# The gated half of the mixed rows: turned by VectorE inside the attention, stored and reloaded turned, with the sums of W_out's blocks moved into the projections

## The chip, the cores and the metric

The kernel runs on one core of one Trainium2 chip. The metric is the device time of one execution in microseconds (us), the median over several. Engines are named as in the profile: PE (TensorE, with PEld for its weight loads), DVE (VectorE), ACT (ScalarE), POOL (GpSimd) and SP (SyncE, which issues most of the DMAs).

## The reference, cut to what matters

One decoder layer over S = 2048 tokens of width D = 1024, all in float32:

```
n = rmsnorm(x);  proj = n @ W_in      # gated q, k, v, gate, low-rank; dilated q, k, v
o_a = gated linear attention, 4 heads of 128, normalised per head, * g * silu(gate)    # S x 512
o_b = dilated attention, 8 heads of 64, three (window, dilation) branches              # S x 512
h = x + [o_a ; o_b] @ W_out
h = h + relu(rmsnorm(h) @ W_ff1)**2 @ W_ff2
y = rmsnorm(h)
```

The change touches how `o_a` travels from the attention to the product with W_out, and where sums of W_out's rows are made for that product.

## The kernel before, in words

**Arithmetic.** Every large product splits both float32 operands into a high part (fp32r) and the rest, and takes three matmuls (`mm3`, L139 to L142). Most products are Strassen-like: seven block products `j` in place of eight, on sums of blocks made by DVE (and by POOL for some weights).

**Stages.** (1) Projections: column groups of W_in, first for tokens 0 to 1023 and then for 1024 to 2047. The loop at L849 runs 126 jobs (group, block product); a group takes seven. A group of 128 columns is "chained" (block products share a PSUM bank) and takes 12 matmuls of 512 columns per job. `prep` (L291) makes a job's weight parts two jobs ahead: ACT writes the high part (L304), DVE the low part (L306, L308), and DVE also makes the sums of blocks (L310 to L316). `load_w` (L284) fetches the next group's weights, through SP for chained groups. `second_half` normalises the second 1024 tokens beside it and turns them with DVE's 32 x 32 block transpose (`squares`, L605); a DMA then puts the blocks in place when they are reloaded (`load_turned`).

(2) Attention: a loop over 160 units of the dilated branches (scores, softmax, transposes, values), PE issuing three units ahead. `gla_steps` (L1161), the gated linear attention, is a generator that is advanced about every second unit; it takes tokens in tiles of 128. In the kernel before, the tokens inside a tile lie in the order 0, 16, 32, ... 1, 17, ... (8 by 16, the function `_order`), and `token_rows` (L144) puts the result rows back in natural order when they are stored in `mixD`. Also in this stage `sum_wo` (L1251, four generators of six steps) loads two row blocks of W_out, has ACT scale the first by the norm's gain (L1257), has POOL make four differences of 128 x 512 (L1261) and stores them in `wtD`.

(3) Product with W_out: `load_mix` (L1467) reads pairs of row tiles from `mixD`; `mix_block` (L1485) turns a row tile by four PE transposes per 512 columns (L1491), so eight for a tile of 1024. The first four row tiles go through `plain_rows` (L1668, ACT and DVE split the turned tile straight from PSUM); for the other twelve, `raw_block` (L1618) has ACT copy the turned tile to SBUF (L1623), `prep0` (L1625) makes the operand parts three jobs ahead, and `product0` (L1654) runs the seven block products of a pair, 12 matmuls each, and has DVE add the result to the residual row (L1664). `row_done` (L1642) stores the row in `hD` and queues `norm_row` (L1410): square and sum on ACT, a scale on DVE that overwrites the row in place (L1415), eight PE transposes (L1420), two ACT copies (L1421), a store in `hTD`.

(4) The MLP's two products, about 1160 us, which the change touches only by calls of `turn_rows`.

**What sets the order.** Each engine runs its instructions in a fixed order, written at compile time by a scheduler that simulates the program: an instruction is placed when, in the simulation, its operands are ready, earlier program lines first. `keep_in_program_order` pins an instruction behind the one traced before it on its engine. SBUF is one pool of 25 slots (`slot`, L127) which tiles take and give back.

## Time and profile before

| | us |
|---|---|
| runs: median of 3 | 2221.89 |
| lowest, highest | 2221.43, 2228.46 |
| the profiled execution | 2219.28 |
| its span, first to last instruction | 2217.1 |

The profiled execution is 2.2 us longer than its span, and 2.6 us under the median. In the profile "busy" counts the time in which an engine has an instruction running; PE's matmuls overlap one another, so what a matmul costs PE is the distance between its start and the next one's, not its duration. A group's row has count, busy time, mean ns of one, and the idle time of the engine just before those instructions with what ended it.

### The profile page before, as it was taken

To read this page: it belongs to the slowest core of one execution; us is meant where nothing else is said; L and a number is where in the kernel's file an instruction comes from. 1 tells how busy PE (TensorE), PEld (TensorE's weight loads), DVE (VectorE), ACT (ScalarE), POOL (GpSimd) and SP (SyncE) were. 2 spreads that over 40 slices of the span, in tenths; PEclk is the share of its full clock that TensorE was granted. 3 is DMA by queue.
4 is the path that set the end of the run, shared out by engine and by line. 5 is a ranking of instruction groups with operands and counts; after the bars stand their busy time and mean duration, and the time that the engine had idled before them with its cause. 6 is when DMAs were issued, how large, how long until landed. Compare 5 with 4: busy or idle time off the path is not lost.

```text
span 2217.1 us, 34928 instructions
## 1 busy us (share of the span) xinstructions
PE 2198.8 (99%) x12356; PEld 1910.1 (86%) x12356; DVE 1662.0 (75%) x3100; ACT 1231.3 (56%) x2406; POOL 604.8 (27%) x653
## 2 busy tenths in 40 slices
PE   9999999999999999999999999999999999999998
PEld 8988998899999998888888888888888888888886
DVE  8677766757777887769776778767786697576788
ACT  7364424537888884547555566555555433333446
POOL 1000300135577672000000000000008443042672
PEclk9999999999999999999999999999999999999999
DMA  6576965777967976868654456555499998677875
GB/s 208 174 218 209 253 204 187 241 243 266 313 231 229 293 262 232 264 212 273 187 167 133 150 180 182 156 177 155 133 299 279 305 297 273 213 258 244 270 263 183
DMA packets 325074, 499.88 MB, mean 225 GB/s; under 512 B 21479, under 2 KB 226938, under 8 KB 313636
## 3 DMA queue, kind: packets, MB, share of 16 engines
q1 hardware_dynamic: 285426, 336.35, 46.8%
q0 software_dynamic: 32128, 108.61, 17.2%
q10 hardware_dynamic: 7346, 52.70, 6.4%
q8 instruction: 97, 1.59, 0.3%
q14 instruction: 77, 0.63, 0.1%
HBM read 339.45 MB, written 162.85 MB: 227 GB/s over the span
## 4 chain that ended last, share of the span: by engine, by line
PE 76%; issue 12%; DMA 4%; DVE 4%; ACT 2%; POOL 1%; SPq 1%; DVEq 0%; POOLq 0%; ACTq 0%
PE ps_a L141 7%; PE ps_a L140 7%; PE ps_a L142 7%; PE ps_c L141 7%; PE ps_c L140 7%; PE ps_c L142 7%; PE ps_a L1021 4%; PE ps_d L141 4%; PE ps_d L142 4%; PE ps_d L140 4%; PE ps_o L140 3%; PE ps_o L141 3%; PE ps_o L142 3%; PE ps_d L1002 3%; PE ps_c L984 2%
## 5 line engine op out<-in xcount | busy, mean ns | idle before, releaser
L543 ACT ACTIVATE cb<-bs 128x1024 fp32r<-128x1024 f32 x104 | 110.2, 1060 | 284.4 <-PE ps_o L141 99.9
L544 DVE TENSOR_TENSOR cb<-bs,cb 128x1024 fp32r<-128x1024 f32 x104 | 150.6, 1449 | 129.0 <-ACT cb L543 128.6
L1508 POOL DMA_DIRECT2D w1raw<-w_ff x64 | 48.0, 750 | 700.3 <-DVE mcomb L544 522.7
L544 DVE TENSOR_TENSOR mcomb<-w1raw,mcomb 128x512 fp32r<-128x512 f32 x224 | 153.4, 685 | 91.4 <-ACT mcomb L543 91.4
L1798 POOL TENSOR_TENSOR bs<-bs,rb 128x1024 f32<-128x1024 f32 x60 | 167.3, 2789 | 199.9 <-DMA bs<-w_ff 196.3
L543 ACT ACTIVATE mcomb<-w1raw 128x512 fp32r<-128x512 f32 x224 | 140.5, 627 | 80.0 <-PE ps_c L142 27.3
L1021 PE MATMUL ps_a<-v,pt 128*128 128x65 f32 x1200 | 177.4, 253 | 2.5 <-ACT pt L1009 1.5
L1021 PEld LDWEIGHTS ps_a<-v,pt 128*128 128x128 f32 x1200 | 172.7, 194 | 4.3 <-ACT pt L1009 1.9
L993 ACT ACTIVATE pe<-pe,O 128x256 f32<-128x256 f32 (+1 forms) x384 | 156.2, 453 | 14.0 <-DVE O L992 11.6
L1002 PE MATMUL ps_d<-ident,pe 128*128 128x128 f32 x600 | 158.4, 279 | 0.2 <-ACT pe L993 0.2
L304 ACT ACTIVATE wcomb<-wraw 128x512 fp32r<-128x512 f32 (+2 forms) x119 | 90.3, 759 | 117.4 <-PE ps_a L141 45.5
L992 DVE CUSTOM_DVE_ANT_0 pe<-ps_c,nb 128x256 f32<-128x256 f32 (+1 forms) x384 | 126.5, 360 | 37.6 <-PE ps_d L1002 18.4
L544 DVE TENSOR_TENSOR ca<-ra,ca 128x1024 fp32r<-128x1024 f32 x84 | 133.6, 1592 | 0.2 <-ACT ca L543 0.2
L140 PE MATMUL ps_c<-hb,mcomb 128*128 128x512 f32 x320 | 124.8, 390 | 0.3 <-ACT xs L1588 0.3
L141 PE MATMUL ps_c<-hb,mcomb 128*128 128x512 f32 x320 | 124.5, 389 | 0.0
L142 PE MATMUL ps_c<-hb,mcomb 128*128 128x512 f32 x320 | 124.2, 389 | 0.0
L140 PE MATMUL ps_c<-cb,ca 128*128 128x512 f32 x312 | 121.4, 389 | 0.0
L141 PE MATMUL ps_c<-cb,ca 128*128 128x512 f32 x312 | 121.4, 389 | 0.0
L142 PE MATMUL ps_c<-cb,ca 128*128 128x512 f32 x312 | 121.4, 389 | 0.0
L1002 PEld LDWEIGHTS ps_d<-ident,pe 128*128 128x128 f32 x600 | 108.3, 185 | 0.6 <-ACT pe L993 0.3
L306 DVE TENSOR_TENSOR wcomb<-wraw,wcomb 128x512 fp32r<-128x512 f32 (+2 forms) x77 | 72.8, 945 | 48.0 <-ACT wcomb L304 47.9
L1579 ACT ACTIVATE acc<-acc 128x512 f32<-128x512 f32 x96 | 60.7, 632 | 79.5 <-DVE acc L1598 37.1
(497 smaller groups left out, 7241.5 us busy)
## 6 DMA issues: line engine op xcount, KB each, us to landing
ra<-actD ACTq DMA_DIRECT2D x50, 1024.0 KB, 7.7
actD<-ring SPq DMA_DIRECT2D x176, 256.0 KB, 3.1
rb<-w_ff POOLq DMA_DIRECT2D x84, 512.0 KB, 6.4
bs<-w_ff SPq DMA_DIRECT2D x72, 512.0 KB, 5.8
w1raw<-w_ff POOLq DMA_DIRECT2D x64, 512.0 KB, 5.2
k<-kD SPq DMA_DIRECT2D x16, 1024.0 KB, 8.0
rb<-hTD SPq DMA_DIRECT2D x28, 512.0 KB, 5.5
wraw<-w_in SPq DMA_DIRECT2D x48, 256.0 KB, 4.0
```

The costliest lines, as they stand in the source:

```text
L140: T.matmul(out, sh, mh, start=first, stop=False, **kw)
L141: T.matmul(out, sl, mh, start=False, stop=False, **kw)
L142: T.matmul(out, sh, ml, start=False, stop=last, **kw)
L304: A.activation(hi, src, AF.Copy, scale=sc)
L306: V.tensor_tensor(lo, src, hi.bitcast(F32), op=OP.subtract)
L543: A.activation(hi, src, AF.Copy)
L544: V.tensor_tensor(lo, src, hi.bitcast(F32), op=OP.subtract)
L992: V.tensor_tensor_reduce(p, s, bias, scale=1.0, scalar=BIG, op0=OP.add, op1=OP.min, accum_out=nm)
L993: A.activation(p, p, AF.Exp, bias=nm, scale=-1.0)
L1002: T.transpose(pb[:, i * 128:i * 128 + 128], src, ident)
L1021: T.matmul(self.b.opsum[:, n % 4], self.pt[:, i * 128:i * 128 + 128], self.b.v[:, blk, cols], start=first, stop=last)
L1798: (engines or ((G,), (V, V))[len(sums) - 1])[e].tensor_tensor(v, v, r, op=OP.add if op == "+" else OP.subtract)
```

## The change

1. The gated attention now works in natural token order inside a tile: `gla_load` and `gla_load_v` read the rows of the gate, v and output gate through `natural_rows`, the constants lose `_order`, and the projected gated q and k (`gq`, `gk`) are put in natural order when they leave PSUM, with the strided form that `dq` had already.
2. At the end of a tile DVE turns the 128 x 512 result in 32 x 32 blocks (`squares`); it is stored in 512-byte runs in the new `mixD`, two tensors of 128 x 16 x 256. The dilated half keeps its natural rows in a tensor of its own, `mixN`.
3. `load_mix` reads the gated half with four DMAs per pair, one for each 32 partitions, in 1 KB runs, which finishes the transposition, and the dilated half with two. The gated half is used from SBUF as it lies (`gated_of`, a strided view); `mix_block` and `raw_block` turn only the dilated half.
4. `sum_wo` moves to the second half of the projections, one generator of four steps per row block on one slot, advanced at the jobs in `SUMS_WO`: 85, 88, 89, 90, then 91, 94, 95, 96, and so on to 108. Its loads are pinned on SP, POOL does the scaling, and POOL issues the store.
5. `norm_row` writes its result in `scr`, not over the row; its transposes are queued and issued by `turn_rows`, called after a block product.

The diff, changed lines with little context:

```diff
@@ -29,6 +29,7 @@
+SUMS_WO = [a + k for a in (85, 91, 97, 103) for k in (0, 3, 4, 5)]
@@ -218,7 +219,8 @@
-    mixD = dram.tile([S, D], F32, name="mixD")
+    mixD = [dram.tile([128, 16, 256], F32, name=f"mixD{h}") for h in range(2)]
+    mixN = dram.tile([S, 512], F32, name="mixN")
@@ -466,7 +468,7 @@
             q = p[:, :m]
-            if kind == "dq":
+            if kind in ("dq", "gq", "gk"):
@@ -844,7 +846,27 @@
+    wtD = dram.tile([4, 128, 2 * D], F32, name="wtD")
+    def sum_wo():
+        raw = slot("wtsum")
+        for c in range(4):
+            for k in range(2):
+                tc.keep_in_program_order(SP.dma_start(raw[:, D * k:D * k + D], wo[:, c + 4 * k]))
+            yield
+            G.tensor_tensor(raw[:, :D], raw[:, :D], gn[:, c:c + 1].to_broadcast([128, D]), op=OP.mult)
+            yield
+            b11, b12, b21, b22 = [raw[:, 512 * k:512 * k + 512] for k in range(4)]
+            for n, (dst, x, y) in enumerate(((b12, b12, b11), (b22, b22, b12), (b21, b21, b22), (b11, b22, b11))):
+                G.tensor_tensor(dst, x, y, op=OP.subtract)
+                if n == 1:
+                    yield
+            G.dma_start(wtD[c], raw[:, :2 * D])
+            yield
+    of_sums = sum_wo()
@@ -863,6 +885,8 @@
             back.pop(0)()
+        if at in SUMS_WO:
+            next(of_sums)
@@ -1080,7 +1104,7 @@
-                        mixD[:, 512 + 128 * pr:640 + 128 * pr].rearrange("(t p) n -> p t n", p=128)[:, ts],
+                        mixN[:, 128 * pr:128 * pr + 128].rearrange("(t p) n -> p t n", p=128)[:, ts],
@@ -1124,18 +1148,21 @@
+    def natural_rows(ap, t, row):
+        return bass.AP(tensor=ap.tensor, offset=ap.offset + t * 128 * row, ap=[[row, 8], [8 * row, 16], [1, row]])
-            SP.dma_start(gst["g"][t % 2], glD[tk])
+            SP.dma_start(gst["g"][t % 2], natural_rows(glD, t, 256))
-            tk = slice(t * 128, t * 128 + 128)
-            SP.dma_start(gst["gv"][t % 2], gvD[tk])
-            SP.dma_start(gst["sr"][t % 2], srD[tk])
+            SP.dma_start(gst["gv"][t % 2], natural_rows(gvD, t, 512))
+            SP.dma_start(gst["sr"][t % 2], natural_rows(srD, t, 512))
@@ -1204,8 +1231,11 @@
             yield
-            V.tensor_tensor(o, o, view(sg, (4, 128)), op=OP.mult)
-            issue_later(4, token_rows(mixD, t, D, width=512), o.rearrange("p h e -> p (h e)"))
+            V.tensor_tensor(view(sg, (4, 128)), o, view(sg, (4, 128)), op=OP.mult)
+            flat = o.rearrange("p h e -> p (h e)")
+            squares(flat, sg)
+            issue_later(4, mixD[t // 8][:, t % 4 * 4:t % 4 * 4 + 4, t % 8 // 4 * 128:t % 8 // 4 * 128 + 128],
+                        view(flat, (4, 128)))
@@ -1246,23 +1276,6 @@
-    wtD = dram.tile([4, 128, 2 * D], F32, name="wtD")
-    def sum_wo(c):
-        raw = slot("wtsum")
-        for k in range(2):
-            SP.dma_start(raw[:, D * k:D * k + D], wo[:, c + 4 * k])
-        yield
-        A.activation(raw[:, :D], raw[:, :D], AF.Copy, scale=gn[:, c:c + 1])
-        yield
-        b11, b12, b21, b22 = [raw[:, 512 * k:512 * k + 512] for k in range(4)]
-        for n, (dst, x, y) in enumerate(((b12, b12, b11), (b22, b22, b12), (b21, b21, b22), (b11, b22, b11))):
-            G.tensor_tensor(dst, x, y, op=OP.subtract)
-            if n < 3:
-                yield
-        issue_later(4, wtD[c], raw[:, :2 * D])
-        yield
@@ -1354,9 +1367,6 @@
-    sums_wo = [x for c in range(4) for x in [sum_wo(c)] * 6]
-    for n, x in enumerate(sums_wo):
-        at_unit(8 + AHEAD + 2 * n, next, x)
@@ -1400,7 +1410,7 @@
-    norms = []
+    norms, turning = [], []
@@ -1412,14 +1422,20 @@
-        V.scalar_tensor_tensor(h, h, r, gM, op0=OP.mult, op1=OP.mult)
-        k = t % HT // 4
-        for q in range(2):
-            pv = view(ps("c"), (4, 128))
-            for c in range(4):
-                T.transpose(pv[:, c], h[:, (4 * q + c) * 128:(4 * q + c + 1) * 128], ident)
-            A.activation(hb4[2 * k + q], pv, AF.Copy)
-        store_T(t, *(((1, 0), (2, 1)) if k == 0 else ((3, 3),)))
+        V.scalar_tensor_tensor(scr, h, r, gM, op0=OP.mult, op1=OP.mult)
+        turning.append(t)
+    def turn_rows():
+        while turning:
+            t = turning.pop(0)
+            k = t % HT // 4
+            for q in range(2):
+                pv = view(ps("c"), (4, 128))
+                for c in range(4):
+                    T.transpose(pv[:, c], scr[:, (4 * q + c) * 128:(4 * q + c + 1) * 128], ident)
+                A.activation(hb4[2 * k + q], pv, AF.Copy)
+            store_T(t, *(((1, 0), (2, 1)) if k == 0 else ((3, 3),)))
@@ -1466,12 +1482,23 @@
-            u = mxs[p] = view(slot("mx"), (2, D))
+            u = slot("mx")
+            mxs[p] = view(u[:, :1024], (4, 256)), view(u[:, 1024:], (2, 512))
+            half, i = divmod(p, 4)
+            to = 384 if half == 0 else 512
+            for g in range(4):
+                m = mixD[half][:, 4 * i + g]
+                SP.dma_start(mxs[p][0][32 * g:32 * g + 32], bass.AP(
+                    tensor=m.tensor, offset=m.offset, ap=[[16 * 256, 32], [32 * 16 * 256, 4], [1, 256]]))
-                to = D - 128 if t < 8 else D
-                for cs in (slice(0, 512), slice(512, to)) if p == 0 else (slice(0, to),):
-                    SP.dma_start(u[:, e, cs], mixD[t * 128:t * 128 + 128, cs])
+                SP.dma_start(mxs[p][1][:, e, :to], mixN[t * 128:t * 128 + 128, :to])
+    def gated_of(p, e):
+        return mxs[p][0].rearrange("p g (e c t) -> p e c g t", e=2, t=32)[:, e]
+    def by_quarter(v):
+        return v.rearrange("p c (g t) -> p c g t", g=4)
@@ -1482,13 +1509,13 @@
-    def mix_block(p, e, q, tag):
+    def mix_block(p, e):
-        pv = view(ps(tag), (4, 128))
+        pv = view(ps("c"), (4, 128))
-            of = mxs[p][:, e, (4 * q + k) * 128:(4 * q + k + 1) * 128]
-            T.transpose(pv[:, k], outs[3, 0][:, t, 1:129] if t < 8 and 4 * q + k == 7 else of, ident)
+            T.transpose(pv[:, k], outs[3, 0][:, t, 1:129] if t < 8 and k == 3 else mxs[p][1][:, e, 128 * k:128 * k + 128],
+                        ident)
@@ -1615,12 +1642,12 @@
-    def raw_block(p, e, q):
+    def raw_block(p, e):
-                raw0.append(view(slot("ar"), (4, 4, 128)))
-            A.activation(raw0[0][:, 2 * e + q], mix_block(p, e, q, "c"), AF.Copy)
+                raw0.append(view(slot("ar", n=1024), (2, 4, 128)))
+            A.activation(raw0[0][:, e], mix_block(p, e), AF.Copy)
@@ -1629,9 +1656,10 @@
-        a11, a12, a21, a22 = [raw0[0][:, n] for n in range(4)]
+        a11, a21 = [gated_of(g // 7, e) for e in range(2)]
+        a12, a22 = [by_quarter(raw0[0][:, e]) for e in range(2)]
-        split(c[:, 0], c[:, 1], {1: a11, 2: a12, 6: a11, 5: a21, 7: a11, 3: a12, 4: a22}[j])
+        split(by_quarter(c[:, 0]), by_quarter(c[:, 1]), {1: a11, 2: a12, 6: a11, 5: a21, 7: a11, 3: a12, 4: a22}[j])
@@ -1647,6 +1675,7 @@
     def next_norm():
+        turn_rows()
@@ -1667,8 +1696,8 @@
-        for q in range(2):
-            split(*[m[:, i, 4 * q:4 * q + 4] for i in range(2)], mix_block(p, e, q, "c"))
+        split(*[by_quarter(m[:, i, :4]) for i in range(2)], gated_of(p, e))
+        split(*[m[:, i, 4:] for i in range(2)], mix_block(p, e))
@@ -1687,8 +1716,8 @@
         if at == 3:
-            for n in range(4):
-                raw_block(2, n % 2, n // 2)
+            for e in range(2):
+                raw_block(2, e)
@@ -1702,6 +1731,7 @@
         next_norm()
+        turn_rows()
@@ -1710,16 +1740,15 @@
         product0(g)
+        turn_rows()
             load_x(p + 1)
-            raw_block(p + 1, 0, 0)
-            raw_block(p + 1, 1, 0)
         if i == 3:
-            raw_block(p + 1, 0, 1)
+            raw_block(p + 1, 0)
         if i == 4:
-            raw_block(p + 1, 1, 1)
+            raw_block(p + 1, 1)
@@ -1888,6 +1917,7 @@
         product1(at)
+        turn_rows()
@@ -1938,11 +1968,6 @@
-def _order():
-    r, i = np.divmod(np.arange(128), 8)
-    return 16 * i + r
@@ -1955,7 +1980,7 @@
-    o = _order()
+    o = np.arange(128)
```

## The prediction

> **What bounds the kernel now.** I read the page first, then the busy time by stage, then PE's own rows where a transposition meets matmuls.

> ```profile
> PE 2198.8 (99%) x12356; PEld 1910.1 (86%) x12356; DVE 1662.0 (75%) x3100; ACT 1231.3 (56%) x2406; POOL 604.8 (27%) x653
> ...
> PE 76%; issue 12%; DMA 4%; DVE 4%; ACT 2%; POOL 1%; SPq 1%; DVEq 0%; POOLq 0%; ACTq 0%
> ```

> PE has work 99% of the time, and most of the chain that ended last is PE. The three stages that the change touches (late projections, attention, product with W_out) are alike in that; the columns are the stretch, its length, then busy time and count for PE, PEld, DVE, ACT, POOL:

> ```profile
> 304.00:505.00 201.00, 201.00 (x1220) 180.34 (x1218) 125.34 (x196) 82.21 (x145) 27.22 (x35) 1.00 0.70 220
> 505.00:842.00 337.00, 334.03 (x3049) 328.52 (x3049) 262.51 (x1050) 291.72 (x845) 239.70 (x321) 1.00 0.82 271
> 842.00:1050.00 208.00, 206.42 (x1029) 171.58 (x1029) 163.98 (x255) 109.19 (x213) 10.53 (x16) 1.00 0.74 239
> ```

> PE idles 0, 3.0 and 1.6 us in them; the granted clock is 1.00. So what leaves PE's queue shortens the kernel, and what is added on other engines costs only where it makes PE wait.

> **The transpositions that go.** A matmul's duration is no price, since matmuls overlap; the price is from start to start. This is one group of eight transposes inside the product with W_out:

> ```profile
> 961.56 1.03 PE L1420 MATMUL ps_c<-ident,xh 128*128 128x128 f32 x8
> ...
> 962.35 0.48 PE L140 MATMUL ps_o<-wo,mcomb 128*128 128x512 f32 x1
> ...
> 962.66 0.40 PE L140 MATMUL ps_a<-wb,mcomb 128*128 128x512 f32 x1
> ...
> 962.90 0.39 PE L141 MATMUL ps_a<-wb,mcomb 128*128 128x512 f32 x1
> 963.13 0.39 PE L142 MATMUL ps_a<-wb,mcomb 128*128 128x512 f32 x1
> ```

> Eight take 962.35 - 961.56 = 0.79 us, 0.099 each. The first matmul after them takes 0.31 to the next start against the usual 0.23, so a group costs 0.08 more however long it is. (Twelve of 0.23 make a product of 2.7 us.) The mixed rows' transposes are of the same form:

> ```profile
> L1491 PE MATMUL ps_c<-ident,mx x120: 270/273/273, 835.8 to 1005.4; 128*128 128x128 f32 x120
> ...
> L1491 PE MATMUL ps_c<-ident,O x8: 270/273/331, 839.6 to 909.9; 128*128 128x128 f32 x8
> ```

> 128 in all, eight for each of 16 row tiles. Half go: 64 x 0.099 = 6.3 us. In the loop over pairs they stand at three places per pair (i = 2, 3, 4) and after the change at two, so six pairs save six groups, 0.5 us. Nothing on PE takes their place. That is 6.8 us.

> [...]

> **What takes over the turning.** DVE's transposition stands in the trace, for 128 x 1024:

> ```profile
> L607 DVE STREAM_TRANSPOSE bp<-xp 128x1024 f32<-128x1024 f32 x8 | 9.9, 1235 | 0.0
> ```

> Half of it, 0.62 us, for 16 tiles is 9.9 us of DVE in the attention, where DVE idles 337 - 262.5 = 74 us and the gated part runs ahead of its use. I take nothing for it; if that cover failed it would cost up to those 9.9 us. The rest is hidden too: the store in 512-byte runs (pair 0 needs only tiles 0 and 4, finished long before), and the reload with six DMAs per pair:

> ```profile
> L1474 SPq DMA_DIRECT2D mx<-mixD x18: 319/423/642, 827.3 to 959.4; - x18
> ...
> DMA to landing us min/median/max: 4.6/5.0/5.3
> ```

> 48 issues in place of 18, 30 x 0.42 = 13 us of SP's queue spread over some 200; they land in 5 us and are issued a pair ahead (seven products). The stores and loads of x behind them on SP slip by about 1.7 us per pair; they too are used a pair later. The twelve ACT copies from PSUM that go (two per pair) are off the path: ACT is busy 109 of 208 us there.

> **Natural order of gq and gk.** Their 28 evictions become strided. The strided form of dq stands in the same rows as the longest value:

> ```profile
> L482 ACT ACTIVATE acc<-ps_a x24: 577/600/1095, 111.9 to 453.9; 128x512 f32<-128x512 f32 x24
> ...
> L492 DVE TENSOR_TENSOR acc<-ps_c,acc x18: 672/692/1067, 112.9 to 451.1; 128x512 f32<-128x512 f32 x18
> ```

> So 0.5 us more on ACT (16 times), 0.4 on DVE (12 times). The bank is written again a whole product later, so PE doesn't see it: 0, at the worst 13 us if all of it lay bare.

> **The norm of h.** The scale no longer overwrites the row, so it no longer waits for the row's store:

> ```profile
> L1415 DVE SCALAR_TENSOR_TENSOR xh<-xh,stats,gs 128x1024 f32<-128x1024 f32 x16 | 20.5, 1280 | 15.9 <-DMA hD<-xh 12.7 <-ACT bb L1421 2.8 <-ACT mcomb L543 0.3
> ...
> L1420 PE MATMUL ps_c<-ident,xh 128*128 128x128 f32 x128 | 16.9, 273 | 0.7 <-DVE xh L1415 0.7
> ```

> 12.7 us of DVE's waiting go; PE waited for it once, 0.7 us. With the transposes queued behind the next product, that goes: 0.7 us. The new wait is that the next row's square may not write `scr` before these transposes have read it; the squares of two rows are two products, 5.4 us, apart and the transposes one product behind the scale, so ACT, where the splits queue behind the square, is not held.

> **The sums leave the attention.** There they cost PE one visible stall:

> ```profile
> 601.19 1.15 ACT L1257 ACTIVATE wtsum<-wtsum,stats 128x1024 f32<-128x1024 f32 x1 [1.25 <-DMA wtsum<-w_out]
> ...
> 602.42 2.65 POOL L1261 TENSOR_TENSOR wtsum<-wtsum 128x512 f32<-128x512 f32 x2 [2.33 <-ACT wtsum L1257]
> ...
> 604.00 1.61 DVE L1207 TENSOR_TENSOR gla<-gla 128x512 f32<-128x512 f32 x1 [1.24 <-ACT gla L1205]
> ...
> 606.94 0.43 PE L1021 MATMUL ps_a<-v,pt 128*128 128x65 f32 x2 [0.76 <-DVE pt L1011]
> ```

> ACT waits for a W_out block, DVE's 128 x 512 operation takes 1.61 us beside POOL's subtraction, and the copy behind it reaches PE late. 0.8 us go.

> **The sums enter the projections.** Per row block POOL does one 128 x 1024 product and four 128 x 512 differences:

> ```profile
> L1798 POOL TENSOR_TENSOR bs<-bs,rb 128x1024 f32<-128x1024 f32 x60 | 167.3, 2789 | 199.9 <-DMA bs<-w_ff 196.3 <-DVE cb L544 3.1
> L1261 POOL TENSOR_TENSOR wtsum<-wtsum 128x512 f32<-128x512 f32 x16 | 20.8, 1315 | 10.2 <-ACT wtsum L1257 10.0
> ```

> 2.8 + 4 x 1.3 = 8 us, four times, 32 us. POOL itself is free there (27 of 201 us). The question is DVE, which makes weight parts beside it, and how early they are:

> ```profile
> L1207 DVE TENSOR_TENSOR gla<-gla x16: 674/718/1606, 546.1 to 840.1; 128x512 f32<-128x512 f32 x16
> ...
> 389.28 0.68 DVE L308 SCALAR_TENSOR_TENSOR wcomb<-wraw,wcomb 128x512 fp32r<-128x512 f32 x1
> ...
> 391.07 0.39 PE L140 MATMUL ps_c<-tb,wcomb 128*128 128x512 f32 x1
> 391.30 0.39 PE L141 MATMUL ps_c<-tb,wcomb 128*128 128x512 f32 x1
> ```

> A DVE operation with both inputs in SBUF that meets POOL takes up to 1.61 in place of 0.67 us. The low part above is done at 389.96 and used at 391.30, 1.3 us early; this is the second job of a group, the tightest. In 8 us DVE is busy 8 x 125/201 = 5.0 us; if two thirds of that are SBUF operations and each doubles, 3.3 us come on top of 3.0 us of slack: nearly level. Bounds: 0, and, if DVE gets none of its SBUF work done while POOL runs, 8 - 3.0 - 1.3 = 3.7 us per block, 15 in all. I take 1.0, near the lower end.

> **The sum.** -6.8 - 0.7 - 0.8 + 1.0 = -7.3 us. The profiled execution took 2219.3 us (span 2217.1 and 2.2 around it), so 2212.0; the median of the runs is 2.6 above that execution, which makes 2214.6.

> **The rivals.**

> *POOL and DVE collide in the projections.* For: the 1.61 us above, and leads of 1.3 us. Against: DVE idles 76 us of the stage and only two jobs of a group are so tight. Between the bounds, about 9 us of stalls: 2221.9 - 8.3 + 9 = 2222.6, no change. [...]

> *SP stands behind a pinned load (the slower case).* One slot serves all four blocks, so block c + 1's load on SP waits until block c's store has landed, and weights of the next group queue behind it on SP:

> ```profile
> 407.62 0.69 DVE L310 TENSOR_TENSOR wraw<-wraw 128x512 f32<-128x512 f32 x1 [1.44 <-DMA wraw<-w_in]
> ```

> ```profile
> wtD<-wtsum SPq DMA_DIRECT2D x4, 1024.0 KB, 8.0
> ...
> wsum<-w_out POOLq DMA_DIRECT2D x4, 512.0 KB, 5.6
> ```

> DVE waits for W_in's blocks already. Load, POOL and store take 5.6 + 8 + 8.0 = 21.6 us per block; the jobs give it six products, 16.3 us. SP would stand 5.3 us for each of three blocks, and if the delay adds up 5.3, 10.6 and 15.9; less 1.3 us of lead each, 12 to 28 us. I price it at the middle, 20: 2221.9 - 8.3 + 20 = 2233.6. It decides where SP waits over 1.3 us with W_in's loads behind, and makes the kernel slower by over 0.3% from 15 us of stalls on. Against: the scheduler places a load when its simulated store has landed, so only its error counts.

> *More than the sum.* The attention loses all its 3.0 us of idle PE and the W_out product its 1.6, with no collision: 2221.9 - 6.8 - 4.6 = 2210.5.

> **How the numbers follow.** A difference of 0.3% (6.7 us, about what a measurement of this kernel can tell from no change) lies just inside my forecast. Chances: the forecast (2211 to 2218) 0.54, collision 0.20, SP's queue 0.14, more than the sum 0.12. Faster by over 0.3% is below 2215.2: 0.12 and three quarters of 0.54, 0.52. Slower is above 2228.6: four fifths of SP's case and a tenth of the collision's, 0.13. The rest, 0.35, is no change. The range 2208 to 2228 leaves out most of SP's case (0.12) and some of the best (0.05).

> **What would show it.** In the changed profile: 64 transposes at the dilated half's line, in groups of four; 16 block transposes of 0.62 us in the attention; no wait for hD's store before the norm's scale; POOL some 32 us busier in the late projections. The product with W_out should be 7 to 8 us shorter, the late projections as long as now. It is wrong if PE shows idle time there that ended with DVE's low parts (collision) or with W_in's loads behind a held SP (queue), or if the attention is over 2 us longer.

## The result, and the profile after

The changed kernel takes 2246.45 us (median of 5 runs, 2243.05 to 2247.61), the kernel before 2222.73 beside it: a ratio of 1.0103, 95% interval 1.0089 to 1.0116. It is 1.0% slower; the forecast was 2214.6 us, 0.3% faster. The profiled execution took 2247.61 us with a span of 2245.8, 28.7 more than before.

The line of busy time and the one of shares by engine of the chain that ended last, of the kernel after:

```profile
PE 2203.6 (98%) x12292; PEld 1912.0 (85%) x12292; DVE 1682.0 (75%) x3116; ACT 1231.0 (55%) x2390; POOL 615.1 (27%) x661
...
PE 72%; issue 14%; DMA 5%; POOL 3%; DVE 3%; ACT 2%; SPq 0%; POOLq 0%; DVEq 0%; ACTq 0%
```

PE has 64 instructions fewer and yet 4.8 us more busy time, and it idles 2245.8 - 2203.6 = 42.2 us instead of 18.3. So there are two questions: who leaves PE 23.9 us more idle, and what makes fewer instructions take longer. The three stages in the same columns as before, now ending at 511, 869 and 1077:

```profile
304.00:511.00 207.00, 202.96 (x1219) 179.99 (x1219) 137.13 (x196) 84.34 (x145) 62.22 (x59) 1.00 0.77 250
511.00:869.00 358.00, 341.11 (x3037) 336.16 (x3037) 268.27 (x1064) 288.98 (x836) 214.09 (x302) 0.96 0.75 231
869.00:1077.00 208.00, 203.87 (x985) 168.36 (x985) 166.46 (x259) 109.49 (x212) 12.75 (x20) 1.00 0.78 246
```

The projections are 6 us longer, the attention 21 us, and its granted clock, 1.00 before, is 0.96. In the third stage PE has 44 instructions fewer for the same 208 us. Around one wait in the attention the clock is seen at work (same columns, a stretch up to the wait's middle and the one behind it), with the matmul that waited:

```profile
785.00:788.20 3.20, 1.11 (x11) 0.92 (x10) 0.62 (x1) 0.00 (x0) 3.20 (x5) 1.00 1.13 277
788.20:798.50 10.30, 8.77 (x45) 8.77 (x46) 5.97 (x27) 7.24 (x20) 7.31 (x15) 0.50 0.38 120
```

```profile
785.21 0.33 PE L1045 MATMUL ps_a<-v,pt 128*128 128x65 f32 x2
785.38 0.28 PE L1026 MATMUL ps_d<-ident,pe 128*128 128x128 f32 x1
785.50 0.61 PE L1172 MATMUL ps_o<-gla 128*128 128x130 f32 x4
789.73 0.69 PE L1045 MATMUL ps_a<-v,pt 128*128 128x65 f32 x2 [3.62 <-DVE pt L1035]
790.21 0.42 PE L1026 MATMUL ps_d<-ident,pe 128*128 128x128 f32 x1
790.43 0.53 PE L1045 MATMUL ps_a<-v,pt 128*128 128x65 f32 x2
790.75 0.42 PE L1026 MATMUL ps_d<-ident,pe 128*128 128x128 f32 x1
```

PE waits 3.62 us, and from then on two values matmuls take 0.32 us to the next start (790.43 to 790.75) where they took 0.17 (785.21 to 785.38). The granted clock is 0.50 for 10.2 us. There are five such stretches in the changed kernel (behind waits at 516, 786, 815, 854 and 1113 us) and none in the kernel before, apart from the very end of both. PE is busy 23.5 us in them, of which half, 11.8 us, is put down to the clock (an estimate from its 0.50). That closes the account: PE's busy time is -6.8 + 11.8 = +5.0 (measured +4.8), its idle time +23.9, together 28.7.

The stages by their own landmarks (start of the matmul named, from the traces; times from the span's start):

| kernel | projections' last | W_out's first | W_out's last | FF1's last | span |
|---|---|---|---|---|---|
| before | 504.7 | 842.0 | 1032.5 | 1647.8 | 2217.1 |
| after | 510.6 | 869.3 | 1053.0 | 1677.0 | 2245.8 |
| norm alone | 504.0 | 841.1 | 1030.5 | 1644.7 | 2215.3 |
| turning alone | 503.6 | 846.3 | 1036.1 | 1654.9 | 2226.8 |
| sums' move alone | 506.7 | 851.5 | 1044.3 | 1660.7 | 2231.5 |
| all but the sums' move | 505.0 | 846.2 | 1031.5 | 1656.9 | 2227.3 |

W_out, first to last, is 190.5 us before and 183.7 after: the 6.8 us of the prediction are there. They are lost ahead of it and behind it: the projections are 5.9 us longer, the attention (from the projections' last to W_out's first) 21.4 us, and FF1, the MLP's first product (from W_out's last to its own last), 8.7 us.

The projections first. Beside POOL's sums (first fence) DVE's 128 x 512 operations (second) take 1.7 us in place of 0.69, and the low part of L308 reaches PE late (third):

```profile
408.19 2.07 POOL L858 TENSOR_TENSOR wtsum<-wtsum,stats 128x1024 f32<-128x1024 f32 x1 [5.37 <-DMA wtsum<-w_out]
410.35 6.72 POOL L862 TENSOR_TENSOR wtsum<-wtsum 128x512 f32<-128x512 f32 x4
```

```profile
412.56 1.67 DVE L318 TENSOR_TENSOR wraw<-wraw 128x512 f32<-128x512 f32 x1
414.15 1.78 DVE L312 TENSOR_TENSOR wraw<-wraw 128x512 f32<-128x512 f32 x1
415.86 1.76 DVE L308 TENSOR_TENSOR wcomb<-wraw,wcomb 128x512 fp32r<-128x512 f32 x1
```

```profile
417.67 0.50 PE L142 MATMUL ps_o<-tb,wcomb 128*128 128x512 f32 x1 [1.22 <-DVE wcomb L308]
```

This is the collision that the prediction priced; the six waits of the stage, five of them ended by DVE, are PE's 4.0 us of idle time in its row above. What it had not seen comes 50 us later, in POOL's queue (first fence), ACT's (second) and PE's (third):

```profile
456.53 2.28 POOL L858 TENSOR_TENSOR wtsum<-wtsum,stats 128x1024 f32<-128x1024 f32 x1 [2.90 <-DMA wtsum<-w_out]
458.88 5.60 POOL L862 TENSOR_TENSOR wtsum<-wtsum 128x512 f32<-128x512 f32 x4
464.78 0.57 POOL L865 DMA_DIRECT2D wtD<-wtsum  x1 [0.30 <-POOL wtsum L862]
465.35 1.55 POOL L286 DMA_DIRECT2D wraw<-w_in  x2
```

```profile
473.12 1.06 ACT L306 ACTIVATE wcomb<-wraw 128x1024 fp32r<-128x1024 f32 x1 [8.14 <-DMA wraw<-w_in]
```

```profile
515.47 0.40 PE L1026 MATMUL ps_d<-ident,pe 128*128 128x128 f32 x2
521.25 0.48 PE L1006 MATMUL ps_c<-k,qp 128*128 128x128 f32 x1 [5.38 <-POOL qp L959]
```

POOL issues the W_in blocks of the last group (256 columns wide). Two of the four stand behind the last block of sums and go out at 465 us; before, the last went out at 458.7. ACT, in order, stands 8.1 us for them; its later evictions, their stores and SP's loads of the bias tables come late, POOL packs q late, and PE waits 5.4 us at the attention's start and then runs 6.8 us at half clock. How much of that wait is due to POOL's queue, e6 and e8 below test.

### The profile page after: what moved, and what is told of

It reads as the page before. It is cut to its first block, busy times and chain, and to the rows that moved or that the text cites. A ratio compares the mean times of both kernels' runs of the same rounds, so it can differ in the third digit from the quotient of the medians.

```text
span 2245.8 us, 34844 instructions
## 1 busy us (share of the span) xinstructions
PE 2203.6 (98%) x12292; PEld 1912.0 (85%) x12292; DVE 1682.0 (75%) x3116; ACT 1231.0 (55%) x2390; POOL 615.1 (27%) x661
## 4 chain that ended last, share of the span: by engine, by line
PE 72%; issue 14%; DMA 5%; POOL 3%; DVE 3%; ACT 2%; SPq 0%; POOLq 0%; DVEq 0%; ACTq 0%
PE ps_a L143 7%; PE ps_a L142 7%; PE ps_a L141 7%; PE ps_c L143 6%; PE ps_c L142 6%; PE ps_c L141 6%; PE ps_a L1045 4%; PE ps_d L142 4%; PE ps_d L141 4%; PE ps_d L143 4%; PE ps_o L141 3%; PE ps_o L143 3%; PE ps_o L142 3%; PE ps_d L1026 3%; PE ps_c L1008 2%
## 5 line engine op out<-in xcount | busy, mean ns | idle before, releaser
L546 DVE TENSOR_TENSOR cb<-bs,cb 128x1024 fp32r<-128x1024 f32 x104 | 157.4, 1515 | 133.5 <-ACT cb L545 133.0
L1045 PE MATMUL ps_a<-v,pt 128*128 128x65 f32 x1200 | 182.1, 255 | 10.7 <-ACT pt L1033 5.2
L1045 PEld LDWEIGHTS ps_a<-v,pt 128*128 128x128 f32 x1200 | 177.6, 197 | 12.7 <-ACT pt L1033 5.4
L306 ACT ACTIVATE wcomb<-wraw 128x512 fp32r<-128x512 f32 (+2 forms) x119 | 90.3, 760 | 117.7 <-PE ps_a L142 42.6
L546 DVE TENSOR_TENSOR ca<-ra,ca 128x1024 fp32r<-128x1024 f32 x84 | 127.3, 1517 | 0.1
L141 PE MATMUL ps_c<-hb,mcomb 128*128 128x512 f32 x320 | 125.4, 392 | 1.7 <-DVE acc L1621 1.7
L142 PE MATMUL ps_c<-hb,mcomb 128*128 128x512 f32 x320 | 125.1, 391 | 0.0
L141 PE MATMUL ps_c<-cb,ca 128*128 128x512 f32 x312 | 121.4, 389 | 0.0
L142 PE MATMUL ps_c<-cb,ca 128*128 128x512 f32 x312 | 121.4, 389 | 0.0
L308 DVE TENSOR_TENSOR wcomb<-wraw,wcomb 128x512 fp32r<-128x512 f32 (+2 forms) x77 | 74.9, 973 | 54.3 <-ACT wcomb L306 54.0
L143 PE MATMUL ps_a<-wcomb,tb 128*128 128x256 f32 (+1 forms) x344 | 97.6, 284 | 0.4 <-DVE stats L557 0.4
## 6 DMA issues: line engine op xcount, KB each, us to landing
ra<-actD ACTq DMA_DIRECT2D x50, 1024.0 KB
rb<-w_ff POOLq DMA_DIRECT2D x84, 512.0 KB, 6.5
bs<-w_ff SPq DMA_DIRECT2D x72, 512.0 KB
w1raw<-w_ff POOLq DMA_DIRECT2D x64, 512.0 KB, 5.1
k<-kD SPq DMA_DIRECT2D x16, 1024.0 KB
rb<-hTD SPq DMA_DIRECT2D x28, 512.0 KB
```

Source lines behind the costliest of these rows:

```text
L141: T.matmul(out, sh, mh, start=first, stop=False, **kw)
L142: T.matmul(out, sl, mh, start=False, stop=False, **kw)
L143: T.matmul(out, sh, ml, start=False, stop=last, **kw)
L306: A.activation(hi, src, AF.Copy, scale=sc)
L308: V.tensor_tensor(lo, src, hi.bitcast(F32), op=OP.subtract)
L546: V.tensor_tensor(lo, src, hi.bitcast(F32), op=OP.subtract)
```

## The experiments

Each ratio is that of the kernel's runs to runs of the kernel before on the same chip, with its 95% interval.

**The parts.** The change falls into three: the sums' move, the norm's part (`scr`, `turn_rows`), and the turning with the natural order, the store and the reload. The first line or two of each:

```diff
 the sums: e1 is the change without them, e2 has them alone
+        if at in SUMS_WO:
+            next(of_sums)
 the norm: e4 has it alone
+        V.scalar_tensor_tensor(scr, h, r, gM, op0=OP.mult, op1=OP.mult)
+        turning.append(t)
 the turning: e5 has it alone
+            SP.dma_start(gst["gv"][t % 2], natural_rows(gvD, t, 512))
+            squares(flat, sg)
```

> The changed kernel with W_out's sums back in the attention (ACT scales, POOL subtracts, four slots), all else changed. Theory A (the sums in the late projections are the cause: POOL collides with DVE there, and the last group's W_in loads stand behind the sums on POOL, which makes the loads for the attention late): the projections end at 505 us as before instead of 511, PE's 5.4 us wait for POOL's packing at the attention's start is gone, and the time falls to 2212 to 2220. Theory B (the turning and its stores in the attention are the cause): the projections end at 505, but PE's long waits later in the attention (3.6, 1.9 and 5.2 us, each followed by some microseconds at half clock) stay, and the time is 2230 to 2240.

> The kernel before with only the move of W_out's sums into the projections. Theory A: the projections end near 511 us and PE waits some 5 us at the attention's start; the time is 2235 to 2250, since nothing is gained elsewhere. Theory B: the move costs the projections up to 6 us and gives back 1 to 3 in the attention: 2222 to 2228.

> The kernel before with only the natural order and the turned, reloaded gated half (no move of the sums, the norm of h as before). Theory A: 64 transposes less on PE and no new wait: 2213 to 2218. Theory B: the product with W_out is 6 to 7 us shorter, but the attention has PE waits of 3 us and more behind a late store or load: 2228 to 2240.

> The kernel before with only the norm of h changed (its result in scr, its transposes queued behind the next block product). Both theories: within 2 us of the kernel before, 0 to 2 us less. If the changed kernel's waits of 1.7 us at the first products of the MLP come from this part, they appear here too and the time is 2224 to 2228.

Measured: all but the sums' move 1.0016 (0.9998 to 1.0034); the sums' move alone 1.0058 (1.0039 to 1.0078); the turning alone 1.0024 (1.0004 to 1.0044); the norm alone 0.9977 (0.9958 to 0.9995). Theory A, the sums, has the larger share, B a smaller one of its own; e1, at 2227.6 us, lies between the two theories' ranges. The norm's part is the only gain, and the one kernel here that beats before. The parts add up to 0.59%; the whole is 1.03%. So some 10 us appear only when they meet, a difference of four measurements that is barely clear of their intervals (about 0.4% together).

**Which side of the sums' move costs.** On the sums' move alone, the last group's W_in blocks were issued by SP (e6), or POOL's five operations a block were left out, so that unsummed blocks are stored (e7). e8 is e6's edit on the whole change.

```diff
 e6, e8
-(SP if g < 2 or chained(g) else G).dma_start(raw_of(...
+(SP if g < 2 or chained(g) or g == 2 * NG - 1 else G).dma_start(raw_of(...
 e7
-G.tensor_tensor(raw[:, :D], raw[:, :D], gn...)
-G.tensor_tensor(dst, x, y, op=OP.subtract)
```

> The sums' move alone, with the last group's W_in blocks (the gated values) issued by SP instead of POOL. Theory C, POOL's queue: in the run of the sums' move alone (2236.9 us) ACT stood 8.0 us before its split at L305 because POOL, busy with the sums, issued the last two of those blocks at 462 us instead of 456 to 459; everything of ACT behind it came late, and PE waited 4.2 us for POOL's packing of q at 512 us and ran 6.8 us at half clock. So the 8.0 us wait shrinks below 2 us, PE's wait and the half clock at 512 us go, and the time falls by 4.2 + 3.4 = 7.6 us to about 2229. Theory D, the collision of POOL's arithmetic with DVE in the projections: the weight parts are as late as before, 2236 within 3.

> The sums' move alone with POOL's five operations per block left out; the loads of W_out and the stores stay where they were, so unsummed blocks are stored. Theory C (POOL's time and queue) and theory D (collision) both say that the projections and the attention's start lose what they had lost: about 2225, 11 us under the run with the arithmetic. Theory G, that the 4 MB of extra transfers on the DMA queues in the late projections are what delays stores and loads: it stays near 2236, with ACT's waits for acc's stores as they were.

> The whole change, with the last group's W_in blocks issued by SP. Theory C: ACT's 8.1 us wait at L306 goes, with it PE's 5.4 us at 521 us and 3.4 of the 6.8 us at half clock: 2246.5 - 8.8 = 2238. If the attention's later waits (785 and 854 us) come of the same lateness, more goes, to about 2230. Theory D: 2246 within 3.

Measured: e6 1.0031 (1.0015 to 1.0047), e7 1.0010 (0.9998 to 1.0022), e8 1.0073 (1.0053 to 1.0094), each beside 1.0058 or 1.0103 without the edit. In e6's trace PE's wait at the attention's start is 0.9 us in place of 4.2, with no half clock there. PE's waits of over 0.2 us in the projections, first in e6, then the only one in the sums' move alone:

```profile
416.70 0.50 PE L142 MATMUL ps_o<-tb,wcomb 128*128 128x512 f32 x1 [1.24 <-DVE wcomb L307]
...
451.34 0.51 PE L141 MATMUL ps_c<-tb,wcomb 128*128 128x512 f32 x1 [1.70 <-ACT wcomb L305]
...
452.81 0.50 PE L142 MATMUL ps_c<-tb,wcomb 128*128 128x512 f32 x1 [0.96 <-DVE wcomb L307]
```

```profile
394.92 0.50 PE L142 MATMUL ps_a<-tb,wcomb 128*128 128x512 f32 x1 [0.47 <-DVE wcomb L309]
```

Without POOL's arithmetic nearly all of the sums' cost is gone (e7's interval holds 1), though its transfers are all there: G falls. About half of the cost, 0.27%, goes when W_in's blocks leave POOL's queue (C); e6's interval and that of the sums' move alone overlap a little. That the other half, 0.21% between e6 and e7, is the collision (D) is argued. For it: the stage's waits end with weight parts, and the projections of the six traces that have the arithmetic at these jobs (the changed kernel, the sums' move alone, e6, e8, e12, e13) are 0.8 to 9.3 us longer than before, 4.9 on the mean. One such trace alone says little: PE waits 3.9 us there in e6 and 0.5 in the sums' move alone. e7's attention, first to last landmark, is 336.0 us against 337.3: the sums' leaving is worth 1.3 us, by these two traces.

In the whole change C holds only in part. In e8 ACT no longer stands for W_in's blocks, and still PE waits at the attention's start, 2.7 us (POOL's queue, then PE's), with 6.8 us of half clock behind it. In e12 and e13 (below), which have e8's order up to there, it waits 4.7 and 5.2 us:

```profile
520.21 0.61 POOL L940 COPY nb<-nb 128x256 f32<-128x256 f32 x1 [12.58 <-DMA nb<-rbD]
```

```profile
521.95 0.47 PE L1006 MATMUL ps_c<-k,qp 128*128 128x128 f32 x1 [2.74 <-POOL qp L959]
```

POOL's packing stands here behind the copy of a bias table, which SP asked for only at 517.8 us (504.9 before). Some kernels with the gated loads in runs of 8 by 16 and no sums in the projections wait at this place too (e18 2.5 us, e1 1.0), the turning alone doesn't. By these traces SP's queue is a second source of the wait, which e8's edit doesn't touch; no run tests it alone.

**Would another place do?** e14 and e17 (with the norm's part) put the sums into the wide jobs, where, as e14's expectation reads the trace of before, the low parts are 3 to 11 us early; e15 does so in the whole change.

```diff
-SUMS_WO = [a + k for a in (85, 91, 97, 103) for k in (0, 3, 4, 5)]
+SUMS_WO = [a + k for a in (64, 67, 70, 73) for k in (0, 1, 1, 2)]
```

> The sums' move alone, but into the wide jobs (64 to 75, at 270 to 342 us), where the trace of before has the low parts of weights 3 to 11 us early. Theory C2, the place is what costs: no PE wait for a low part while POOL sums, no late W_in blocks of the gated values, the attention starts as before; 2222 within 3, 14 us under the narrow place (2236.9). Theory M, the sums cost in the projections wherever they stand, or by having left the attention: over 2230.

> The whole change with the sums in the wide jobs. Theory C2, and the rest of the loss follows from the late start of the attention: it costs what the change without the sums' move costs, 2227.6 within 3, 19 us under the whole change. Theory Q, the turning and the emptied attention collide by themselves (the waits at 785 and 854 us stay): 2237 within 4.

> The norm's part (2219.5 us alone) and the sums in the wide jobs, no turning. Theory C2: the attention loses the one stall of the sums, 0.8 us: 2218.5 within 3, the fastest kernel here. Theory M: 2228 or more.

Measured: e14 1.0074 (1.0056 to 1.0092), e15 1.0114 (1.0095 to 1.0134), e17 1.0056 (1.0041 to 1.0072). Theory C2 was wrong. M's time came, over 2230 us, but not by what cost in the narrow place: no low part is late beside the sums. It is the mechanism of the prediction's second rival that has come. SP's queue in e14, and what DVE and PE waited for:

```profile
311.81 10.11 SPq L285 DMA_DIRECT2D wraw<-w_in  x4
328.67 0.82 SPq L855 DMA_DIRECT2D wtsum<-w_out  x2
329.59 11.93 SPq L285 DMA_DIRECT2D wraw<-w_in  x3
```

```profile
336.17 1.28 DVE L311 TENSOR_TENSOR wraw<-wraw 128x512 f32<-128x512 f32 x1 [6.80 <-DMA wraw<-w_in]
...
350.80 0.69 DVE L311 TENSOR_TENSOR wraw<-wraw 128x512 f32<-128x512 f32 x1 [7.71 <-DMA wraw<-w_in]
```

```profile
353.59 0.41 PE L347 MATMUL ps_d<-ident,misc 128*50 128x128 f32 x1 [5.92 <-DVE misc L345]
```

What SP stood for in e14 before such loads, L855, from 290 to 362 us (us in total, times, longest):

```profile
SPq L855 <- DMA wtD<-wtsum: 8.7, 2, 6.7
```

The first narrow group's weights come through SP and stand behind the pinned load of a sums' block, which itself waits up to 6.7 us until the block before has been stored. This is read from the trace; no run takes the wait away. In e15 PE's wait at the attention's start is 1.5 us, with no half clock behind it, and the late waits stay, 3.6 us at 789 and 4.3 at 856, as theory Q says, at a time 10 us over Q's. Wherever the sums were put, one of the two queues that bring W_in's blocks, POOL's or SP's, had a part of them ahead of those loads.

**What of the turning costs.** e9 is the turning alone without VectorE's transposition (the gated rows are stored and reloaded unturned). e16 is the natural order alone. e18 and e19 are its two halves, each with the gated q and k in another order than the values.

```diff
 e9, on the turning alone
-V.tensor_tensor(view(sg, (4, 128)), o, view(sg, (4, 128)), op=OP.mult)
-squares(flat, sg)
+V.tensor_tensor(o, o, view(sg, (4, 128)), op=OP.mult)
 e18, on before (e19 has only the other line; e16 both)
-SP.dma_start(gst["gv"][t % 2], gvD[tk])
+SP.dma_start(gst["gv"][t % 2], natural_rows(gvD, t, 512))
 e19
-if kind == "dq":
+if kind in ("dq", "gq", "gk"):
```

> The turning alone without VectorE's transposition: the gated rows are stored unturned in the new layout and reloaded as the change does, natural order of gq and gk included. Theory E, the 16 transpositions and what stands behind them on DVE cost the 6 us of the turning alone (2229.1): about 2223. Theory F, the strided evictions, the store and the six reloads per pair cost them: stays at 2229 within 3, with the waits for hD's store at 930 us and for the W_out block at 603 us as in the turning alone.

> Only the natural order of rows in the gated part: strided evictions of its q and k, loads in 8 by 16 runs, the causal mask's order, a contiguous store; no turning by VectorE, the product with W_out as before. Theory N, the natural order is what the turning alone costs (2229.1): 2229 within 3, with PE waits in the attention. Theory R, it is the split store and the reload by six transfers a pair, by way of SP and the wait for h's store: 2222 within 3.

> The natural order with the evictions of the gated q and k left as before (so q and k stand in another order than the values, and the output is not the reference's): only the loads of the gated rows in runs of 8 by 16 and the contiguous store are new. Theory S, the strided evictions cost: 2222 to 2224, as before. Theory T, the loads and the order that the scheduler makes of them cost: 2229 within 3, with the waits at 607 and 780 us.

> Only the 28 strided evictions of the gated q and k (again in another order than the values, so the output is not the reference's); all else is as before and in the same order on every queue but for these. Theory S: 2229 within 3. Theory T, and the prediction's own term (0 us, as the bank is not written again for a whole product): 2222 to 2224.

Measured: e9 1.0055 (1.0036 to 1.0073), e16 1.0034 (1.0018 to 1.0049), e18 1.0036 (1.0020 to 1.0052), e19 1.0000 (0.9983 to 1.0017). VectorE's 16 transpositions are not the cost: without them the kernel is no faster, by the medians slower than either theory gave (PE waits 2.2 and 2.8 us for the norm's scale at 900 and 939 us, waits of the kind that the norm's part is meant to remove). The strided evictions cost nothing (e19). e18 has all of the cost: the loads of the gated rows in runs of 8 by 16, and with them the contiguous store, whose issue got shorter (0.38 us at 588 us, against 0.56). The order of its instructions is that of before on PE, DVE and POOL, and on SP but for a few DMAs that changed places. SP's issue of the gate's rows, in e19 (as before) and in e18 (ns, shortest, median and longest):

```profile
L1130 SPq DMA_DIRECT2D gla<-glD x14: 319/326/588, 508.0 to 771.4; - x14
```

```profile
L1134 SPq DMA_DIRECT2D gla<-glD x14: 575/596/618, 510.0 to 781.4; - x14
```

An issue takes 0.60 us where it took 0.33 (for v and the output gate, 16 each, the medians go from 0.48 and 0.55 to 0.59 and 0.60). That is little, but SP is what the others stand behind. The load of a W_out block for the sums at 590 us, and ACT's wait for it, first in e19, then in e18:

```profile
588.59 6.57 SPq L1255 DMA_DIRECT2D wtsum<-w_out  x2
```

```profile
599.80 1.15 ACT L1257 ACTIVATE wtsum<-wtsum,stats 128x1024 f32<-128x1024 f32 x1 [0.17 <-DMA wtsum<-w_out]
```

```profile
592.06 9.32 SPq L1258 DMA_DIRECT2D wtsum<-w_out  x2
```

```profile
606.26 1.15 ACT L1260 ACTIVATE wtsum<-wtsum,stats 128x1024 f32<-128x1024 f32 x1 [3.74 <-DMA wtsum<-w_out]
```

Behind ACT's 3.74 us the softmax's evictions are late and PE waits 2.0 and 0.9 us at 607 and 611 us, then 6.8 us at half clock; PE also waits 2.5 us at 508 and 1.6 at 842 us. Why the two issues at 592 us took 9.3 and not 6.6 us the trace doesn't say. In the changed kernel this load of W_out isn't in the attention; what the slower issues cost there was not measured by itself.

**Is the saved PE time real, and what eats it at FF1?** On all but the sums' move, e10 issues the dilated half's 64 transposes twice over into the same bank; e11 asks for the first two blocks of W_ff1 four products earlier.

```diff
 e10
-for k in range(4):
+for k in [*range(4)] * 2:
 e11
-if g in (49, 53):
+if g in (45, 49):
```

> The change without the sums' move (2227.6 us), with the dilated half's 64 transposes issued twice over into the same bank: PE has the number of transposes of before again, 6.3 us more; the computation is the same. Theory H, the gain is given back at the handover to FF1: in that kernel DVE reaches FF1's first sum of weights, stands 5.5 us for the W_ff1 block at 1005 us, is then busy 19 of 20 us, and PE waits 1.5 + 1.8 + 0.6 us for it; so PE's saved time was not on the path and the 6.3 us cost less than 2: 2229.5 or less. Theory P, the product is bound by PE and the saved 6.8 us are real, other things lose the time: 2227.6 + 6.3 = 2234.

> The change without the sums' move, with the first two loads of W_ff1's blocks asked for four products earlier. Theory H: DVE's 5.5 us stand at the first sum of weights shrinks, and with it PE's waits at the handover (about 4 us) and the 2.3 us and half clock near 1093: about 2221, 6 to 7 us under 2227.6. Theory P (the block's load has nothing to do with it): 2227 within 3.

Measured: e10 1.0033 (1.0016 to 1.0050), e11 0.9997 (0.9983 to 1.0011), against 1.0016. In e10 W_out takes 192.4 us in place of 185.3: that product is bound by PE, and the 6.8 us are real in it. For the whole kernel neither theory is shown. e10 is 0.17%, 3.8 us, slower than the kernel without the repetition, between P's 6.3 and H's 2 and inside the intervals; of the 6.1 us by which its span is longer, 3.5 lie in the attention, where the edit does nothing. And FF1 takes 622.2 us in place of 625.4: some of what W_out gains is given back at the handover, as H says. In all but the sums' move, DVE there:

```profile
1004.50 0.69 DVE L1665 TENSOR_TENSOR mx<-ar,mx 128x512 f32<-128x512 f32 x1
1010.70 0.69 DVE L1544 TENSOR_TENSOR w1raw<-w1raw 128x512 f32<-128x512 f32 x1 [5.50 <-DMA w1raw<-w_ff]
```

FF1's first 300 matmuls take 8.5 us longer than before in that kernel, 7.3 in the whole change, 1.7 with the norm alone. In e11 DVE waits 2.9 us in place of 5.5 and the first 100 matmuls lose 0.5 us in place of 3.6, but a wait of 2.75 us with half clock stays at 1091 us. The gain, 0.19%, is too small for these intervals.

**The two late waits of the attention.** On e8, e12 loads W_out's last two blocks three units earlier, e13 stores the dilated pairs' rows one unit earlier.

```diff
 e12
-at_unit(NU - 28 + 3 * i + AHEAD, load_wo, ...
+at_unit(NU - 28 + 3 * i + AHEAD - (3 if i > 5 else 0), load_wo, ...
 e13
-issue_later(3 if pr < 3 else 2, mixN...
+issue_later(2, mixN...
```

> The whole change with the gated values' W_in blocks on SP (2240.3 us), and the loads of W_out's last two blocks three units earlier. Theory J, in the last part of the attention ACT stands 4.8 us for a W_out block that SP, itself standing for a store of a branch's output, issues at 850 us, PE waits 4.8 to 5.2 us at 854 and runs at half clock: that goes, 4.8 + 1.7 to 3.4 us, to about 2233. Theory K, the attention's end is late whatever that block does (the branch's outputs themselves are late): 2240 within 3.

> The whole change with the gated values' W_in blocks on SP (2240.3 us), and the store of each dilated pair's rows issued one unit earlier. Theory L, at 773 us that store is issued late behind the turned gated rows' store, POOL stands 11.6 us for its landing before it may pack q, the gated part behind it on POOL is late, DVE with it, and PE waits 3.6 us at 787 and runs 6.8 us at half clock: that goes, 3.6 + 3.4 us, to about 2233. Theory K, the place only moves: 2240 within 3.

Measured: e12 1.0078 (1.0055 to 1.0102), e13 1.0073 (1.0047 to 1.0098), against 1.0073. In e12 the wait at 854 us is gone and no half clock follows:

```profile
844.86 0.43 PE L1045 MATMUL ps_a<-v,pt 128*128 128x65 f32 x2 [1.23 <-DVE pt L1035]
...
847.02 0.44 PE L1045 MATMUL ps_a<-v,pt 128*128 128x65 f32 x2 [0.75 <-ACT pt L1033]
```

So the wait's cause is as J says, and the time doesn't fall: W_out takes 187.4 us, 3.8 more than e8's 183.6, and FF1 2.7 more. e13's edit changed the order of no engine: instruction for instruction its queues are e8's, so it is e8 measured a second time, and L was not tested.

## Why the prediction was wrong

**Where it failed.** The step is the place of the sums in the projections, "I take 1.0, near the lower end", with "POOL itself is free there (27 of 201 us)". The sums' move alone costs 0.58%, 13 us, and 0.10% without POOL's arithmetic. Of the 13 us some 5 are put down to the collision that the text described (e7 against e6, and the projections' mean), between its 1.0 and its upper bound of 15. DVE's added work was sized well: 3.3 us per block, 13.2 in all, where its busy time in the stage grew by 11.8 (137.1 against 125.3 us). What failed is to set it off against the slack of the stage's mean, for the weight parts that meet POOL are late all the same. About half, 6 us, follows from reading "free" off a busy share. POOL's 27 busy us are not what matters in that queue; four issues of 0.8 us are, for ACT stands for their landing, and the last two, issued at 456.0 and 458.7 us in the kernel before, went out at 465.4 and 466.1 in the changed one, behind 2.28 and 5.60 us of sums.

**What had no term.** (1) The loads of the gated rows in runs of 8 by 16: under "Natural order" only the evictions were priced (rightly at 0, by e19). They cost 0.36%, 8 us, on the kernel before (e18). (2) The clock: a wait was counted at its length. In the changed kernel an estimated 11.8 us are lost at half clock behind waits of 1.7 to 5.4 us. (3) The handover to FF1: DVE stands for W_ff1's block (5.5 us in all but the sums' move), and FF1 is 8.7 us longer in the changed kernel; what makes it so was not settled.

**What was right.** 64 transposes and 6.8 us in W_out (183.7 against 190.5 us; e10 shows their price in that stage). VectorE's turning hidden: 16 of 0.706 us against the estimate of 0.62, at no cost (e9). The norm's new scale: DVE's 12.7 us of waiting for the row's store are gone, and the norm alone gains 0.23%, 5 us (0.05 to 0.42%; its trace is 1.8 us shorter), rather than 0.7. The sums' leaving the attention: 1.3 us against 0.8.

**The rivals.** The collision happened, with less than half of the sums' loss; its price of 9 us was high, as the 1.0 of the sum was low: the runs give some 5. The prediction's 15 us was its estimate for the case that DVE gets none of its SBUF work done while POOL runs. In the changed kernel's trace DVE lost less: beside POOL's four operations (6.72 us from 410.35 us on) three of DVE's were done from 412.56 to 417.62, in 1.67 to 1.78 us each, about as long as one of POOL's, and the cost stayed under the bound. SP behind a pinned load did not decide in the changed kernel: SP stands 12.9 us for the blocks' stores there, in three waits, but DVE's waits for W_in's blocks are 6.3 us against 8.4 before. In e14 it did, one place further.

**What stays open.** Some 10 us, 0.44%, appear only when the parts meet. 0.15% of it is there when the norm's part and the turning meet without the sums' move (1.0016, where the two alone add up to 1.0001); by the table FF1 then takes 625.4 us, against 614.2 with the norm alone and 618.8 with the turning alone. The rest comes when the sums join, by the table in the attention: 21.4 us there, where all but the sums' move has 3.9 and the sums' move alone 7.5. Two of the waits in which they lie, 3.6 us at 786 and 5.2 at 854, are in every trace that has both the turning and the sums' move (in e12 only the first, of 1.95 us). With the sums' move alone PE has no wait over 1.1 us there, with parts of the turning shorter ones (2.7 us at 781 in e16). What brings them was not settled: taking one away (e12) did not shorten the kernel.

## What to carry to other kernels

Before something is put on an engine that looks idle, list what is already queued there and who waits for it: here four DMA issues counted, not POOL's 174 idle microseconds. Price every DMA whose shape changes, its issue time on the queue too (0.33 to 0.60 us here), not only the work for which it is changed. And where PE carries the kernel, price a wait of two microseconds at more than two: here each of PE's 36 pauses of 2.0 us or more was followed by 3.41 to 10.24 us at half clock.

## What the runs showed of the hardware

**The same instructions, other times.** e8 and e13 have the same order on every engine from first to last, e12 the same up to the late attention, and their last matmul of the projections started at 514.0, 509.8 and 505.5 us; PE waited 5.2, 3.8 and 0.6 us in that stage. So the same instructions in the same order differed by up to 8.5 us in when this stage ended, more than e6's edit, 6 us, is worth. That POOL's and DVE's operations meet at other places each time would explain it, but was not shown.
